# A three-block network on one core: the head steps of the first mixers cut into short pieces, VectorE bound to the planner's order, products placed behind every second dense step, and weights beyond seven fetched later

## The chip, the core and the metric

The kernel runs on one core of a Trainium2 chip, in one launch. What counts is the time of that core on the device, in microseconds (us). Engines: TensorE (PE in the profile; PEld is its weight load), VectorE (DVE), ScalarE (ACT), GpSimd (POOL) and SyncE (SP), which issues the weight transfers.

## What is computed

Three blocks follow each other on a sequence of 512 positions with 1024 channels, all in 32-bit floats: a block with two mixers (a gated delta rule on four heads and a retention on four heads) and a convolutional MLP, then a block of sliding-window attention with pooling, then a gated convolution block. The change touches the first mixers, and a little of the passage into the last block.

```python
proj = rms_norm(h, attn_norm_w) @ w_in            # 36 tiles of 128 columns
q, k, v = split(silu(causal_conv4(...)))          # gated delta rule, 4 heads of 128
q, k = l2norm(q) * d**-0.5, l2norm(k)
m = where(strict, (k*beta) @ k.T * decay, 0)      # per chunk
t_mat = solve_triangular(eye + m, eye)            # unit lower triangle
u_base, w_mat = t_mat @ (v*beta), t_mat @ (k*beta*exp(gcum))
qk = (q @ k.T) * decay
# scan over the chunks:
u = u_base - w_mat @ S;  o = (q*exp(gcum)) @ S + qk @ u;  S = S*cd + k_dec.T @ u
o = rms(o) * norm_w * silu(gate)                  # per head
# retention, 4 heads: rotary q, k; o = rms(retention(q, k, v)) * silu(gate)
h = h + concat(o_gdn, o_ret) @ w_out
```

## The kernel before

**Dense products.** Activations lie channels by positions. Each 32-bit factor is split into a high and a low part, and a dense product is three matmuls of 128x512 (`mm3`, lines 330 to 332). A projection tile is eight dense steps (k = 0 to 7) of three matmuls (`side_steps`). Weights come by SP into three buffers (`raw`); ScalarE makes the high part (`whi`, or `op` where buffers are lent), VectorE or GpSimd the low part (`unpack`, `prefetch`).

**First mixers.** While the 36 projection tiles go through TensorE, the heads' own small products are put between the dense steps. A head of the delta rule is a generator, `gdn_head`: sums of squares (L704) and transposes of k (L686); the norms on VectorE (`rsqrt_small`, some ten tiny operations, each needing the one before); the products k·k (L732) and q·k (L734), which VectorE turns into `Mt` and `At` with four SCALAR_TENSOR_TENSOR each; the triangular inverse by doubling, two batches of 16 tiny products (L759) per level with VectorE between them; then the scan over four chunks (L831, L832, L842, L848, L855), in which VectorE makes `ru` and the state. `finish_head` normalizes a head's result, again with a chain of tiny operations, `ret_head` is a retention head.

**The planner.** A loop written in the kernel sets the order. It keeps a clock of its own: a dense step adds 0.64 to it, a head's step adds the cost that it yields, and the step after it is ready once the clock has passed the latency that it yields (`need(n, lat, cost)`; the constants `L_PRE`, `L_NORM`, `L_M` and so on). A ready step goes ahead of the next dense step. The order so made is binding for PE and SP alone (`manual_schedule`); what stands on VectorE, ScalarE and GpSimd is ordered by the framework's scheduler. A step's instructions on an engine run in the order in which they stand there, whatever is ready.

```python
ready = [e for e in live if e[0] <= clock[0]]
if ready: step(ready[0])
elif main ...: clock[0] += next(main)             # one dense step
else: clock[0] = min(e[0] for e in live)
```

**Passage into the last block.** The output product of the second block runs in two halves of the positions; `p6_norm` is a chain of norms for each half (squares, a row sum on TensorE at L1275, a reciprocal root, then 8 tiles scaled), while the first seven tiles of the last block's weights (`N_FIRST`) are used on the other half. `prefetch` takes further weights as buffers come free.

Of the kernel before, what the change touches and what calls it, by code (L numbers as in the profile page):

```python
# [41 lines left out]
L_NORM = 15  # L42
L_M = 5.8
# [113 lines left out]
def build(tc, xT, par, cst, rope, w_ab, w_in, w_rv, w_out, w_up, w_down, a_w, ab_w, c_w, co_w, post1, poolw, out, dbg=None):  # L157
# [134 lines left out]

    def prefetch(ins=None):
# [46 lines left out]
    credit = [0.0]  # L340
# [15 lines left out]
    def side_steps(ws, X, sl=slice(0, T), ab=None):  # L356
# [6 lines left out]
        for k in range(KD):  # L363
# [57 lines left out]
    def rsqrt_small(y, x, n, tag):  # L421


        h, t = small(n, tag + "l"), small(n, tag + "t")
# [8 lines left out]


# [222 lines left out]
    def finish_head(i, scale, wn):  # L657
# [3 lines left out]
        so, ms, r = small(NCH, "so"), small(NCH, "oms"), small(NCH, "or")  # L661
# [3 lines left out]
        fr(junk)  # L665
        if scale is not None:
# [3 lines left out]
        rsqrt_small(r, ms, NCH, "ors")  # L670
# [3 lines left out]
        yield from need(1, L_FIN)  # L674
# [14 lines left out]
    def gdn_head(h, qT, kT, vT):  # L689
# [16 lines left out]
        sse = sp.tile([128, 2, 4], F32, tag="sse", name="sse")  # L706
        rn = sp.tile([128, 2, 4], F32, tag="rn", name="rn")
# [5 lines left out]
        rsqrt_small(rn.rearrange("p a c -> p (a c)"), sse.rearrange("p a c -> p (a c)"), 8, "rn")  # L713
# [13 lines left out]
        pm.fr(pv)  # L727
        fr(vT)
# [8 lines left out]
        for c in range(NCH):  # L737
            STT(At[:, ch(c)], pkq[:, ch(c)], f[:, c:c + 1], Ec[:, ch(c)], MUL, MUL)
        pm.fr(pk, pkk, pkq)
        fr(Ec, Es)  # L740
# [10 lines left out]
        gps.memset(Tf, 0.0)  # L751
        TT(vc(Tt, c32), vc(Mc, c32), bc4(cc("lev", 0, c32)), MUL)
# [9 lines left out]
        cost = 2.2  # L762
        for n in range(1, 5):
            yield from need(1, L_M if n == 1 else L_T, cost)
# [5 lines left out]
            yield from need(1, L_Z, cost)  # L770
# [160 lines left out]

    def step(e):

        try:
            cost, lat = next(e[1])
            clock[0] += cost
            e[0] = clock[0] + lat
        except StopIteration:
# [820 lines left out]
```

## Time and profile before

| what | value |
|---|---|
| median of 3 runs | 1109.29 us (1107.78 to 1110.65) |
| the profiled execution | 1109.99 us, span 1108.2 us |
| PE busy in the span | 1081.0 us, 98% |
| DVE, ACT, POOL busy | 759.6, 508.5, 200.8 us |
| granted TensorE clock, mean | 0.994 of full speed |
| transfers | 96.04 MB, mean 87 GB/s |

The span runs from the first instruction to the last. A busy PE is not a PE at its peak: matmuls are pipelined, each is shown as 0.39 us long while the next starts 0.23 us later, so waits are read from the starts. In a row of the timeline the first number is the start in us from the span's start, the second the duration, then come engine, line, operation, tiles written and read, the shape, the count, and in brackets the idle time before it with what ended it. Lines are those of the kernel before; in the changed kernel they stand 2 to 20 lines further down (L704 is L714, L686 is L696, L732 is L742, L754 is L762, L759 is L767, L709 is L720).

### The profile page before, as it was taken

Reading aid. Unit: us, or ns where it says so; the run is one execution under the profiler, and the core shown is the slowest. Engines: PE = TensorE matmul, PEld = TensorE weight load, DVE = VectorE, ACT = ScalarE, POOL = GpSimd, SP = SyncE. Lnnn points to the kernel's source line nnn. Section 1 sums busy time; section 2 is a strip of 40 time slices with the busy share of each in tenths; the row PEclk is TensorE's granted clock in tenths of the full one; section 3 lists DMA queues with packets and bytes.
Section 4 is the critical chain, followed back from the end, with each engine's and each line's share of the span. In section 5 each row is a group of like instructions: output and inputs, shape, how many; then the busy total and the mean of one; then the engine's idle time right before and its main releaser. Section 6 shows DMA issues by size and latency. Waiting matters only on the chain.

```text
span 1108.2 us, 17712 instructions
## 1 busy us (share of the span) xinstructions
PE 1081.0 (98%) x6902; PEld 871.6 (79%) x6902; DVE 759.6 (69%) x1522; ACT 508.5 (46%) x1017; POOL 200.8 (18%) x194
## 2 busy tenths in 40 slices
PE   7998989999999999999999999999999999999997
PEld 5876778788888888888888888766789996665886
DVE  7787566577567877676663234668855857989855
ACT  6742444215344544443453245355445546544542
POOL 0931222101030000000000016000000003999100
PEclk9998999999999999999999999999999999999999
DMA  8321112114232333333333333211232403111021
GB/s 287 120 78 55 40 59 77 59 38 134 77 114 76 114 95 96 98 104 103 95 96 93 100 96 106 77 58 39 77 95 76 153 23 113 57 59 60 18 76 76
DMA packets 28947, 96.04 MB, mean 87 GB/s; under 512 B 3552, under 2 KB 3808, under 8 KB 28864
## 3 DMA queue, kind: packets, MB, share of 16 engines
q1 hardware_dynamic: 27936, 91.90, 26.3%
q0 software_dynamic: 928, 3.02, 0.9%
q8 instruction: 54, 0.88, 0.3%
q14 instruction: 29, 0.24, 0.1%
HBM read 92.81 MB, written 2.10 MB: 86 GB/s over the span
## 4 chain that ended last, share of the span: by engine, by line
PE 88%; DVE 8%; ACT 1%; DMA 1%; issue 1%; SPq 0%; DVEq 0%; ACTq 0%
PE bank L330 26%; PE bank L331 25%; PE bank L332 25%; DVE act L175 2%; PE bank L1443 2%; DVE act L178 2%; PE bank L1149 1%; PE bank L759 1%; PE bank L1187 1%; DVE bank L178 1%; DVE wlo L175 1%; PE bank L1176 1%; PE bank L1427 1%; PE bank L438 1%; DMA raw<-in_c_w_dram 1%
## 5 line engine op out<-in xcount | busy, mean ns | idle before, releaser
L330 PE MATMUL bank<-op,whi 128*128 128x512 f32 (+1 forms) x575 | 224.1, 390 | 5.8 <-ACT whi L171 5.8
L332 PE MATMUL bank<-op,wlo 128*128 128x512 f32 (+1 forms) x575 | 217.6, 378 | 0.0
L331 PE MATMUL bank<-op,whi 128*128 128x512 f32 (+1 forms) x575 | 217.5, 378 | 0.0
L330 PE MATMUL bank<-op,op 128*128 128x512 f32 (+1 forms) x538 | 207.2, 385 | 0.4 <-ACT stk L171 0.4
L331 PE MATMUL bank<-op,op 128*128 128x512 f32 (+1 forms) x538 | 202.5, 376 | 0.0
L332 PE MATMUL bank<-op,op 128*128 128x512 f32 (+1 forms) x538 | 202.0, 375 | 0.0
L171 ACT ACTIVATE op<-raw 128x512 fp32r<-128x512 f32 (+1 forms) x168 | 102.3, 625 | 144.1 <-PE bank L331 117.2
L171 ACT ACTIVATE whi<-raw 128x512 fp32r<-128x512 f32 (+1 forms) x158 | 96.2, 622 | 127.0 <-PE bank L331 120.5
L175 DVE TENSOR_TENSOR op<-raw,op 128x512 fp32r<-128x512 f32 (+1 forms) x140 | 97.0, 705 | 68.3 <-ACT op L171 67.9
L330 PEld LDWEIGHTS bank<-op,whi 128*128 128x128 f32 x575 | 109.5, 190 | 29.5 <-ACT whi L171 6.0
L332 PEld LDWEIGHTS bank<-op,wlo 128*128 128x128 f32 x575 | 109.4, 190 | 20.4 <-DVE wlo L175 0.4
L331 PEld LDWEIGHTS bank<-op,whi 128*128 128x128 f32 x575 | 109.7, 191 | 19.6 <-issue 1.9
L175 DVE TENSOR_TENSOR wlo<-raw,whi 128x512 fp32r<-128x512 f32 (+1 forms) x129 | 91.8, 717 | 43.6 <-ACT whi L171 43.2
L330 PEld LDWEIGHTS bank<-op,op 128*128 128x128 f32 x538 | 101.5, 189 | 24.4 <-issue 4.3
L332 PEld LDWEIGHTS bank<-op,op 128*128 128x128 f32 x538 | 101.4, 188 | 18.6 <-issue 0.6
L331 PEld LDWEIGHTS bank<-op,op 128*128 128x128 f32 x538 | 101.5, 189 | 17.4 <-issue 1.3
L171 ACT ACTIVATE act<-act 128x512 f32<-128x512 f32 (+3 forms) x113 | 56.2, 506 | 77.3 <-DVE act L175 23.0
L175 POOL TENSOR_TENSOR act<-act,act 128x512 f32<-128x512 f32 x57 | 78.8, 1390 | 28.1 <-ACT act L171 26.6
L175 DVE TENSOR_TENSOR bank<-bank,act 128x512 f32<-128x512 f32 x56 | 38.6, 695 | 52.3 <-PE bank L332 52.1
L330 PE MATMUL bank<-whi,op 128*128 128x512 f32 (+1 forms) x199 | 73.4, 369 | 0.4 <-DVE act L175 0.4
L332 PE MATMUL bank<-whi,op 128*128 128x512 f32 (+1 forms) x199 | 72.6, 365 | 0.0
L331 PE MATMUL bank<-wlo,op 128*128 128x512 f32 (+1 forms) x199 | 72.3, 363 | 0.0
(362 smaller groups left out, 1650.5 us busy)
## 6 DMA issues: line engine op xcount, KB each, us to landing
raw<-in_w_up_dram SPq DMA_DIRECT2D x44, 512.0 KB, 3.5
raw<-in_w_in_dram SPq DMA_DIRECT2D x25, 512.0 KB, 3.6
raw<-in_c_w_dram SPq DMA_DIRECT2D x24, 512.0 KB, 3.7
raw<-in_a_w_dram SPq DMA_DIRECT2D x18, 512.0 KB, 3.4
raw<-in_w_down_dram SPq DMA_DIRECT2D x16, 448.0 KB, 3.3
raw<-in_w_out_dram SPq DMA_DIRECT2D x8, 512.0 KB, 3.5
raw<-in_w_down_dram SPq DMA_DIRECT2D x8, 512.0 KB, 3.5
raw<-in_ab_w_dram SPq DMA_DIRECT2D x8, 512.0 KB, 3.4
```

Of the source, the lines that this page charges most:

```text
L171: last[0] = act.activation(out=out, in_=in_, func=func, **k)
L175: return (e or dve).tensor_tensor(out=out, in0=in0, in1=in1, op=o)
L178: return (e or dve).scalar_tensor_tensor(out=out, in0=in0, scalar=scalar, in1=in1, op0=o0, op1=o1)
L330: pe.matmul(ps, lhsT=l[0], rhs=r[0], start=first, stop=False)
L331: pe.matmul(ps, lhsT=l[0], rhs=r[1], start=False, stop=False)
L332: pe.matmul(ps, lhsT=l[1], rhs=r[0], start=False, stop=last)
L438: pe.matmul(p, lhsT=ones, rhs=ss, start=True, stop=True)
L759: pe.matmul(p[pt(i), c * c32:(c + 1) * c32], lhsT=l[pt(i), c * c32:(c + 1) * c32], rhs=r[pt(i), c * c32:(c + 1) * c32], start=True, stop=True)
L1149: pe.matmul(v2(psc[e])[:, i, lo:], lhsT=qT[sl, ch(b)], rhs=kT[sl, (b - 1) * C + lo:(b + 1) * C], start=True, stop=True)
L1176: pe.transpose(v2(pt)[:, i, ch(j)], sc[:, i, ch(j)], ident)
L1187: pe.matmul(po[64 * e:64 * e + 64, ch(b)], lhsT=vtok[:, kb * C + 64 * e:kb * C + 64 * e + 64], rhs=v2(pT)[:, i, ch(j)], start=j == 0 or b ...
L1443: pe.matmul(acc[32 * q:32 * q + 32], lhsT=wds[m][i // 4][:, i % 4 * C + 32 * q:i % 4 * C + 32 * q + 32], rhs=st[:, o:o + T], start=i == 0, ...
```

## The change

The latencies of two steps are shortened (15 to 4.0 and 5.8 to 2.0). The chains of tiny operations become steps of their own (`rsqrt_steps`), which yield a third number and so count as steps without products. `step` queues each step's VectorE instructions behind those of the step before, so the planner's order binds VectorE for the heads' steps; the evacuations of the dense tiles and the weights' low parts stay with the scheduler. `grain` is true after every second dense step, and a step with products waits for that. In `gdn_head` the product q·k with its four VectorE operations moves from ahead of the inverse into its first level, and v's scaling moves behind the diagonal's preparation. `cap` stops `prefetch` at seven weights of the last block until the second half begins. No product, transfer or element of work is added or taken away; tiny tiles get four buffers where they had two.

```diff
-L_NORM = 15
-L_M = 5.8
+L_NORM = 4.0
+L_M = 2.0
...
-        while nxt[0] < len(stream) and len(his.free) >= 2 * len(landing) + 2 and raws.free:
+        while nxt[0] < cap[0] and len(his.free) >= 2 * len(landing) + 2 and raws.free:
...
@@ side_steps
+            grain[0] = k % 2 == 1 or len(ws) > 1
             yield 0.64 * len(ws)
...
-    def rsqrt_small(y, x, n, tag):
+    def rsqrt_steps(y, x, n, tag, bufs=2):
...
         TT(h, t, x, MUL)
+        yield
         STT(t, h, -10.0 / 3.0, h, ADD, MUL)
...
@@ finish_head
         fr(junk)
+        yield 0.0, 2.2, 0
...
-        rsqrt_small(r, ms, NCH, "ors")
+        for _ in rsqrt_steps(r, ms, NCH, "ors", 4):
+            yield 0.0, 1.2, 0
+        yield 0.0, 1.0, 0
...
-        yield from need(1, L_FIN)
+        yield from need(1, L_FIN - 6.0)
...
@@ gdn_head
+        yield 1.0, 0.4, 0
...
-        rsqrt_small(rn.rearrange("p a c -> p (a c)"), sse.rearrange("p a c -> p (a c)"), 8, "rn")
+        for _ in rsqrt_steps(rn.rearrange("p a c -> p (a c)"), sse.rearrange("p a c -> p (a c)"), 8, "rn", 4):
+            yield 0.0, 2.0, 0
+        yield 0.0, 1.0, 0
...
-        yield from need(3, L_NORM, 2.2)
+        yield from need(2, L_NORM)
...
-        TT(v4(vr), v4(pv), b3(rki), MUL)
...
-        pkk, pkq = pm(), pm()
+        pkk = pm()
...
-        for c in range(NCH):
-            pe.matmul(pkq[:, ch(c)], lhsT=kT[:, ch(c)], rhs=qT[:, ch(c)], start=True, stop=True)
+        yield 1.3, 0.3, 0
...
+        TT(v4(vr), v4(pv), b3(rki), MUL)
...
+            if n == 1:
+                pkq = pm()
...  (q·k and its four VectorE operations)
+            yield from need(1, L_Z, 1.4 if n == 1 else cost)
...
@@ step
+        n = len(tc.nc.cur_bb.bb.instructions)
+        with contextlib.ExitStack() as behind:
+            if turn[0] is not None:
+                behind.enter_context(tc.issue_after(turn[0]))
...
+        for i in tc.nc.cur_bb.bb.instructions[n:]:
+            if i.engine == mybir.EngineType.DVE:
+                turn[0] = i
...
-        ready = [e for e in live if e[0] <= clock[0]]
+        ready = [e for e in live if e[0] <= clock[0] and (grain[0] or not e[3])]
...
+    cap[0] = len(stream) - co_w.shape[0] - c_w.shape[0] + N_FIRST
     start_chain(0)
```

How the order changes is shown at three places. **First, TensorE where heads 0 and 1 make their products of keys.** `bank` is an accumulator, `stk` and `act` are activations, `ck` the identity. Before:

```order
L686 MATMUL bank_165<-ck,stk_95 128x128 x4
L732 MATMUL bank_163<-stk_96 128x128 x4
L734 MATMUL bank_159<-stk_95,stk_96 128x128 x4
L330 MATMUL bank_160<-op_111,whi_143 128x512
L331 MATMUL bank_160<-op_112,whi_143 128x512
L332 MATMUL bank_160<-op_111,wlo_153 128x512
L704 MATMUL bank_165<-act_70,ck 32x128 x4
```

Now:

```order
L696 MATMUL bank_163<-ck,stk_95 128x128 x4
L742 MATMUL bank_165<-stk_96 128x128 x4
L332 MATMUL bank_160<-op_105,whi_143 128x512
L333 MATMUL bank_160<-op_106,whi_143 128x512
L334 MATMUL bank_160<-op_105,wlo_153 128x512
L332 MATMUL bank_160<-op_107,whi_143 128x512
L333 MATMUL bank_160<-op_108,whi_143 128x512
L334 MATMUL bank_160<-op_107,wlo_153 128x512
L696 MATMUL bank_159<-ck,stk_95 128x128 x4
L742 MATMUL bank_162<-act_86 128x128 x4
```

q·k (L734) is gone from behind k·k, six matmuls (two dense steps) stand between the two heads, and both heads' k·k now stand ahead of the sums of head 2. Head 0's first batch of the inverse (L759, now L767) has 78 dense matmuls ahead of it since the tile of q2 began, before and now; its second batch has 87 before and 90 now; head 0's second level begins after 96 in both.

**Second, VectorE ahead of the first batches of the inverse.** `act_76` is head 0's diagonal and the matrices made of it, `act_82` head 1's; `act_75` and `stk_96` are `Mt` of heads 0 and 1, `act_74` is `At` of head 0, `wlo` a weight's low part. Before, up to head 0's transposition (L754):

```order
L175 TENSOR_TENSOR act_73<-bank_165,rki 128x512
L178 SCALAR_TENSOR_TENSOR act_75<-bank_163,f,act_84 128x128 x4
L178 SCALAR_TENSOR_TENSOR act_74<-bank_159,f,act_78 128x128 x4
L175 TENSOR_TENSOR act_76<-act_76,act_93 128x128
L709 STREAM_TRANSPOSE act_70<-bank_165 128x256
L175 TENSOR_TENSOR act_76<-act_76,ck 128x128
L175 TENSOR_TENSOR wlo_152<-raw_136,whi_142 128x512
L754 STREAM_TRANSPOSE act_76<-act_76 128x128
```

Now, up to the same transposition (L762), and then the end of the list up to head 1's:

```order
L178 SCALAR_TENSOR_TENSOR act_75<-bank_165,f,act_85 128x128 x4
L178 SCALAR_TENSOR_TENSOR stk_96<-bank_162,f,act_89 128x128 x4
L175 TENSOR_TENSOR act_76<-act_76,act_93 128x128
L175 TENSOR_TENSOR act_73<-bank_163,rki 128x512
L175 TENSOR_TENSOR act_76<-act_76,ck 128x128
L175 TENSOR_TENSOR bank_160<-bank_160,act_67 128x512
L762 STREAM_TRANSPOSE act_76<-act_76 128x128
```

```order
L175 TENSOR_TENSOR act_76<-bank_162,act_93 128x128
L178 SCALAR_TENSOR_TENSOR act_74<-bank_163,f,act_78 128x128 x4
L175 TENSOR_TENSOR act_82<-act_82,act_93 128x128
L175 TENSOR_TENSOR stk_96<-bank_159,rki 128x512
L175 TENSOR_TENSOR act_82<-act_82,ck 128x128
L178 SCALAR_TENSOR_TENSOR rnt<-rnl 128x8
L175 TENSOR_TENSOR wlo_154<-raw_137,whi_144 128x512
L762 STREAM_TRANSPOSE act_82<-act_82 128x128
```

`At` of head 0 (made of q·k), the sums of head 2 (L709) and one low part have moved from ahead of head 0's transposition to behind it; `Mt` of head 1 and an evacuation (`bank_160`) have moved ahead of it. Between the two lists stand head 2's sums, that low part, three operations of a convolution and five tiny ones.

**Third, VectorE in the scan, where heads finish.** `or`, `orst`, `orsl` are the tiny tiles of `finish_head`, `rn`, `rnt` those of head 3's norms; the row with `neg` makes `ru`, which TensorE's next product awaits. Before:

```order
L178 SCALAR_TENSOR_TENSOR orst<-orst,oms 128x4
L175 TENSOR_TENSOR orst<-or 128x4
L178 SCALAR_TENSOR_TENSOR rn<-rnt,rn 128x8
L178 SCALAR_TENSOR_TENSOR or<-orst,or 128x4
L178 SCALAR_TENSOR_TENSOR orst<-orst,oms 128x4
L175 TENSOR_TENSOR rnt<-rn 128x8
L175 TENSOR_TENSOR or<-or,cq 128x4
L178 SCALAR_TENSOR_TENSOR or<-orst,or 128x4
L178 SCALAR_TENSOR_TENSOR rnt<-rnt,sse 128x8
L175 TENSOR_TENSOR act_89<-act_89,or 128x512
L178 SCALAR_TENSOR_TENSOR rn<-rnt,rn 128x8
L178 SCALAR_TENSOR_TENSOR stk_95<-bank_165,neg,act_78 128x128
```

Now:

```order
L175 TENSOR_TENSOR stk_95<-stk_95,bank_163 128x128
L175 TENSOR_TENSOR rki<-sse,rn 128x4
L175 TENSOR_TENSOR f<-rn 128x4
L182 TENSOR_SCALAR cq<-rn 128x4
L175 TENSOR_TENSOR f<-f,beta 128x4
L175 TENSOR_TENSOR fl<-f,ge 128x4
L175 TENSOR_TENSOR stk_96<-bank_165,fl 128x512
L175 TENSOR_TENSOR so<-so,cq 128x4 x2
L182 TENSOR_SCALAR oms<-so 128x4
L182 TENSOR_SCALAR orst<-oms 128x4
L182 TENSOR_SCALAR or<-orst 128x4
L175 TENSOR_TENSOR orst<-or 128x4
```

Before, two finishing heads and head 3's norms lie interleaved ahead of one `ru`; now they come one after the other, half a chain at a time, with the scan's operations between the pieces.

## Rows read from the trace of the kernel before

**Rows 1.** The page: busy time by engine, its share of the span, and instructions.

```profile
PE 1081.0 (98%) x6902; PEld 871.6 (79%) x6902; DVE 759.6 (69%) x1522; ACT 508.5 (46%) x1017; POOL 200.8 (18%) x194
```

**Rows 2.** Waits of TensorE over the whole span: line, what ended them, us in total, times, longest.

```profile
PE bank L759 <- DVE act L175: 4.4, 1, 4.4
PE bank L842 <- DVE f L175: 3.6, 1, 3.6
PE bank L1275 <- DVE act L175: 2.0, 1, 2.0
PE bank L704 <- ACT act L171: 1.5, 2, 1.2
PE bank L759 <- DVE act L776: 1.2, 1, 1.2
PE bank L759 <- issue: 0.5, 1, 0.5
```

**Rows 3.** Stretches of the span: from and to, length, busy us (and instructions) of PE, PEld, DVE, ACT and POOL, then the granted clock, the share of the DMA engines and GB/s.

```profile
60.50:81.40 20.90, 19.36 (x136) 16.02 (x135) 18.74 (x56) 8.48 (x16) 5.75 (x6) 1.00 0.23 73
84.40:88.80 4.40, 0.10 (x1) 0.00 (x0) 4.40 (x23) 2.95 (x7) 0.71 (x2) 0.79 0.00 2
88.80:93.80 5.00, 4.95 (x59) 3.56 (x62) 2.51 (x6) 0.03 (x1) 0.93 (x1) 0.50 0.31 108
105.90:120.00 14.10, 12.43 (x401) 9.64 (x387) 10.58 (x28) 4.58 (x10) 4.07 (x10) 1.00 0.27 78
153.90:158.60 4.70, 0.73 (x4) 0.30 (x2) 4.70 (x22) 1.61 (x2) 2.11 (x3) 1.00 0.00 0
158.60:162.10 3.50, 3.44 (x11) 2.86 (x11) 1.93 (x6) 0.80 (x2) 0.00 (x0) 0.51 0.45 145
874.00:890.00 16.00, 13.96 (x112) 13.60 (x111) 12.67 (x33) 5.88 (x15) 0.00 (x0) 1.00 0.54 165
```

**Rows 4.** TensorE's timeline where heads 0 and 1 make their products.

```profile
74.02 1.06 PE L732 MATMUL bank<-stk 128*128 128x128 f32 x8
74.91 1.06 PE L734 MATMUL bank<-stk,stk 128*128 128x128 f32 x8
...
81.78 0.45 PE L759 MATMUL bank<-act 32*32 32x32 f32 x32
...
83.88 0.39 PE L331 MATMUL bank<-op,whi 128*128 128x512 f32 x1
84.11 0.39 PE L332 MATMUL bank<-op,wlo 128*128 128x512 f32 x1
88.85 0.65 PE L759 MATMUL bank<-act 32*32 32x32 f32 x32 [4.36 <-DVE act L175]
...
93.57 0.63 PE L759 MATMUL bank<-act 32*32 32x32 f32 x41
```

**Rows 5.** VectorE's timeline in the same stretch.

```profile
76.07 2.15 DVE L178 SCALAR_TENSOR_TENSOR act<-bank,f,act 128x128 f32<-128x128 f32 x8
...
79.73 1.35 DVE L175 TENSOR_TENSOR wlo<-raw,whi 128x512 fp32r<-128x512 f32 x1 [0.35 <-ACT whi L171]
81.00 0.30 DVE L754 STREAM_TRANSPOSE act<-act 128x128 f32<-128x128 f32 x1
...
83.85 0.74 DVE L178 SCALAR_TENSOR_TENSOR stk<-bank,pr,stk 128x510 f32<-128x510 f32 x1
...
88.32 0.28 DVE L175 TENSOR_TENSOR act<-act,act 128x128 f32<-128x128 f32 x1
88.52 0.28 DVE L175 TENSOR_TENSOR act<-bank,act 128x128 f32<-128x128 f32 x1
88.72 1.16 DVE L175 TENSOR_TENSOR act<-act,ck 128x128 f32<-128x128 f32 x1
```

**Rows 6.** GpSimd's timeline in this stretch.

```profile
88.39 1.34 POOL L175 TENSOR_TENSOR wlo<-raw,whi 128x512 fp32r<-128x512 f32 x1 [3.10 <-ACT whi L171]
```

**Rows 7.** VectorE's timeline in the scan.

```profile
151.96 1.20 DVE L175 TENSOR_TENSOR rnt<-rn 128x8 f32<-128x8 f32 x1
...
157.31 0.33 DVE L178 SCALAR_TENSOR_TENSOR stk<-bank,neg,act 128x128 f32<-128x128 f32 x1
```

**Rows 8.** ScalarE's timeline in the scan.

```profile
149.22 1.28 ACT L171 ACT_TABLE_LOAD   x1
150.52 0.60 ACT L171 ACTIVATE act<-bank 128x512 f32<-128x512 f32 x1
...
151.48 0.31 ACT L171 ACTIVATE act<-stk 128x128 f32<-128x128 f32 x1
151.70 0.19 ACT L171 ACTIVATION_READ_ACCUMULATOR act<-stk 128x1 f32 x1
```

**Rows 9.** VectorE's timeline in the passage into the last block, second half of the positions.

```profile
879.10 0.17 DVE L175 TENSOR_TENSOR qt<-qy 128x8 f32<-128x8 f32 x1
879.30 0.17 DVE L175 TENSOR_TENSOR qt<-qt,qx 128x8 f32<-128x8 f32 x1
...
881.80 1.29 DVE L175 TENSOR_TENSOR op<-raw,op 128x512 fp32r<-128x512 f32 x2 [2.14 <-ACT op L171]
883.02 0.44 DVE L455 STREAM_TRANSPOSE act<-qy 128x256 f32<-128x256 f32 x1
883.49 6.32 DVE L175 TENSOR_TENSOR act<-act,act 128x256 f32<-128x256 f32 x18
```

More of the change, by code (lines that the diff above doesn't have):

```diff
@@ L291, in unpack @@
         made.append(w)
+    cap = [len(stream)]
     def prefetch(ins=None):
@@ L338, in build @@
     pend = collections.deque()
-    credit = [0.0]
+    credit, grain = [0.0], [True]
     def tick(n=RATE):
@@ L419, in rsqrt_guess @@
         TS(y.bitcast(I32), t.bitcast(I32), -1.0, MUL, float(0x5F3759DF), ADD)
-    def rsqrt_small(y, x, n, tag):
-        h, t = small(n, tag + "l"), small(n, tag + "t")
+    def rsqrt_steps(y, x, n, tag, bufs=2):
+        h, t = small(n, tag + "l", bufs), small(n, tag + "t", bufs)
         rsqrt_guess(y, x, t)
@@ L432, in rsqrt_small @@
         STT(y, t, 9.0 / 16.0, y, ADD, MUL)
+    def rsqrt_small(*a):
+        for _ in rsqrt_steps(*a):
+            pass
     def row_sums(ss):
@@ L660, in finish_head @@
         o, scale = O[i], scale and scale()
-        so, ms, r = small(NCH, "so"), small(NCH, "oms"), small(NCH, "or")
+        so, ms, r = (small(NCH, n, 4) for n in ("so", "oms", "or"))
         junk = al()
@@ L705, in gdn_head @@
         pk = transpose4(kT)
-        sse = sp.tile([128, 2, 4], F32, tag="sse", name="sse")
-        rn = sp.tile([128, 2, 4], F32, tag="rn", name="rn")
+        sse = sp.tile([128, 2, 4], F32, tag="sse", name="sse", bufs=4)
+        rn = sp.tile([128, 2, 4], F32, tag="rn", name="rn", bufs=4)
+        yield 1.0, 0.4, 0
         st = sq[0][:, :256]
@@ L722, in gdn_head @@
         TT(v4(kd), v4(pk), b3(fl), MUL)
-        yield from need(3, L_NORM, 2.2)
+        yield from need(2, L_NORM)
         pv = transpose4(vT)
         vr = al()
-        TT(v4(vr), v4(pv), b3(rki), MUL)
-        pm.fr(pv)
-        fr(vT)
         At, Mt = al(), al()
-        pkk, pkq = pm(), pm()
+        pkk = pm()
         for c in range(NCH):
             pe.matmul(pkk[:, ch(c)], lhsT=kT[:, ch(c)], rhs=kT[:, ch(c)], start=True, stop=True)
-        for c in range(NCH):
-            pe.matmul(pkq[:, ch(c)], lhsT=kT[:, ch(c)], rhs=qT[:, ch(c)], start=True, stop=True)
+        yield 1.3, 0.3, 0
         for c in range(NCH):
             STT(Mt[:, ch(c)], pkk[:, ch(c)], f[:, c:c + 1], Es[:, ch(c)], MUL, MUL)
[L737 to L740, printed above, removed]
+        pm.fr(pk, pkk)
+        fr(Es)
         c32, g4 = C // 4, range(4)
@@ L751, in gdn_head @@
         gps.memset(Tf, 0.0)
+        yield 0.0, 2.8, 0
         TT(vc(Tt, c32), vc(Mc, c32), bc4(cc("lev", 0, c32)), MUL)
@@ L760, in tiles @@
                               rhs=r[pt(i), c * c32:(c + 1) * c32], start=True, stop=True)
-        cost = 2.2
+        TT(v4(vr), v4(pv), b3(rki), MUL)
+        pm.fr(pv)
+        fr(vT)
+        cost = 0.0
         for n in range(1, 5):
-            yield from need(1, L_M if n == 1 else L_T, cost)
+            yield from need(2 if n == 1 else 1, L_M if n == 1 else L_T, cost)
             cost = 0.5
@@ L769, in gdn_head @@
             pm.fr(pz)
-            yield from need(1, L_Z, cost)
+            if n == 1:
+                pkq = pm()
+                for c in range(NCH):
+                    pe.matmul(pkq[:, ch(c)], lhsT=kT[:, ch(c)], rhs=qT[:, ch(c)], start=True, stop=True)
+                for c in range(NCH):
+                    STT(At[:, ch(c)], pkq[:, ch(c)], f[:, c:c + 1], Ec[:, ch(c)], MUL, MUL)
+                pm.fr(pkq)
+                fr(Ec)
+            yield from need(1, L_Z, 1.4 if n == 1 else cost)
             pb = pm()
@@ L930, in start @@
         wait.append((g, key, after))
+    turn = [None]
     def step(e):
[L934 to L938, printed above, removed]
-            live.remove(e)
-            if e[2] is not None:
-                done.add(e[2])
+        n = len(tc.nc.cur_bb.bb.instructions)
+        with contextlib.ExitStack() as behind:
+            if turn[0] is not None:
+                behind.enter_context(tc.issue_after(turn[0]))
+            try:
+                cost, lat, *vec = next(e[1])
+                clock[0] += cost
+                e[3] = not vec
+                e[0] = clock[0] + lat
+            except StopIteration:
+                live.remove(e)
+                if e[2] is not None:
+                    done.add(e[2])
+        for i in tc.nc.cur_bb.bb.instructions[n:]:
+            if i.engine == mybir.EngineType.DVE:
+                turn[0] = i
     def admit():
@@ L948, in admit @@
                 wait.remove(x)
-                live.append([0.0, x[0], x[1]])
+                live.append([0.0, x[0], x[1], False])
                 step(live[-1])
@@ L1033, in build @@
                 main = None
+                grain[0] = True
         else:
             clock[0] = min(e[0] for e in live)
+            grain[0] = True
     order.close()
@@ L1370, in p7_units @@
                 lazy[0] = False
+                cap[0] = len(stream)
                 order.close()
```

1 line of the change is left out of this document (added).

## Prediction

> **What bounds the kernel now.** I read the page first: TensorE is busy 98% of the span [rows 1], so only its waits, its clock and the room between its matmuls can give time. The list of its waits comes next [rows 2]. The change reaches six of them: 4.4 and 1.2 us at the batches of the inverse (L759) and 0.5 more there, 3.6 at the scan (L842), 1.5 in two waits at the sums (L704), and 2.0 at the row sum of the passage into the last block (L1275). Third, the stretches [rows 3]: the 4.4 us wait is followed by 5.0 us at a granted clock of 0.50, the wait at L842 by 3.5 us at 0.51, which is the lower of the two levels. All other rows of the stretches, with waits of 1.2, 0.5 and 2.0 us in them, have 1.00. So a long wait is paid twice: about 5.0 x 0.5 = 2.5 us behind the first, 3.5 x 0.49 = 1.7 behind the second. Fourth, who makes TensorE wait: in both long waits VectorE is busy for the whole stretch (4.40 of 4.40 and 4.70 of 4.70), and from 60.5 to 81.4 it is busy 18.74 of 20.90 [rows 3]. VectorE, not TensorE, sets the pace between about 60 and 91 us. That is what the reader should take along: an order on TensorE helps there only as far as VectorE's list up to the awaited result gets shorter.
>
> **The change part by part.** No work is added, so each term is a wait that goes or comes. I follow VectorE's list to the next result that TensorE awaits.
>
> *Head 0's first batch.* Before, VectorE ends the transposition at 81.30 [rows 5] and TensorE starts the batch at 81.78 without a wait [rows 4]. Now the list up to it lacks four of eight SCALAR_TENSOR_TENSOR (2.15 / 8 = 0.27 each, 1.07), a low part (1.27, from 79.73 to 81.00 [rows 5]) and a transposition of 256 columns (0.44 shown [rows 9], 0.36 with the overlap below). It has four more of head 1's `Mt` (1.07) and an evacuation of 512 columns, like a low part that nothing hinders (0.6). Net: 1.0 shorter. A part of VectorE's own idle time is filled too; I take 0.4. So the result is ready near 79.9. TensorE comes earlier by more: two q·k (0.89 each by k·k's starts, 74.02 to 74.91 [rows 4]) stand behind this point now, and the 1.5 us at L704 [rows 2] belong to a silu that VectorE finishes sooner against TensorE's order. It would be there at 81.8 - 1.8 - 1.5 = 78.5. New wait: 1.4, in one piece or split with the sums of head 2.
>
> *Head 1's first batch.* Behind it VectorE has, in order: a transposition 0.44, a low part 0.68, three conv operations of 0.74 [rows 5], five tiny ones of which two hide (3 x 0.20, by the starts 879.10 and 879.30 [rows 9]), the level's mask 0.28, `At` 1.07, three of 0.28, 0.68 and 0.28 for head 1, a tiny one, a low part 0.68 and the transposition 0.30. That is 7.7 as shown; operations start about 0.08 before the one ahead is shown to end (88.32 + 0.28 against 88.52 [rows 5]), 14 times, so 6.6. GpSimd makes two low parts meanwhile. Its operation at 88.39 took 1.34 [rows 6], and a VectorE operation that began at 88.72 then took 1.16 where two like it took 0.28 [rows 5]: 0.9 lost. Two such make 1.8 at most, none at least. I take 1.1, so 7.7: ready at 87.6 (86.5 to 88.3). TensorE has a batch 0.45, q·k 0.89, twelve dense matmuls at 0.23 (83.88 to 84.11 [rows 4]) and a batch, 4.6 in all, and is there at 84.5. New wait: 3.1 (2.0 to 3.8). After it a batch, q·k and six dense matmuls, 2.7, bring head 0's second level to 90.3. Before, that level began at 93.57 [rows 4] with the same 96 dense matmuls and both q·k behind it, and head 1's batch (0.45) still to come. Gain 3.7, if the clock stays up. A wait of 3.1 lies between the 2.0 that left the clock at 1.00 and the 4.4 and 3.6 that did not, nearer to 3.6. So in the forecast it falls, and I charge 2.1, the middle of 2.5 and 1.7. **Gain here 1.6** (1.0 to 4.5).
>
> The Trainium skill (SBUF — State Buffer, section "Who interferes with whom") says that VectorE's second read interface is shared with GpSimd and locked for a whole instruction: a VectorE operation with two inputs in SBUF waits until a GpSimd operation that reads SBUF has ended, or the other way round. The 1.16 us beside the 1.34 us agree. By the page alone each GpSimd operation can cost up to its full 1.34 us; for the five of the two stretches that is up to 6.7 in place of the some 2 us in my terms, and the sum would come out at a gain near 2.
>
> *Later levels.* Between 93.8 and 120 the two waits of 1.2 and 0.5 [rows 2] stood behind VectorE's convolution and norm operations. Now every result there has two or four dense steps (1.4 or 2.7 us) of TensorE's time to be made in, against one to three operations of 0.2 to 0.74. **Gain 1.7** (0.5 to 1.7).
>
> *The scan.* Before, `ru` at 157.31 [rows 7] had some thirty tiny operations of three chains ahead of it, one of them 1.20 long under a GpSimd operation [rows 7]. Its wait, 3.6 at L842 and 0.4 before the next dense matmul, 4.70 - 0.73 = 4.0 by the stretch, and the clock's 1.7 go [rows 3]: 5.7. What comes: ScalarE's list holds two Squares (0.31 and 0.19 each), a silu like the 0.60 of a 512-column row, the table load 1.28, an exponential 0.60 and a copy 0.3 [rows 8], 3.8, against 3.8 of TensorE's (decays, sums, transposes, a piece of the scan, two dense steps): 0 to 0.7 wait; three more Squares then 0.3; VectorE's piece of head 3's norms and of a finish ahead of `ru`, twelve tiny ones at 0.20 and one of 0.68, 3.1, against 1.7 of TensorE's and a head start of some 0.5: 0.9, and up to 2 with a GpSimd operation in it; an accumulator that comes free late, 0.4. With the clock kept, since dense steps lie between them, 2.5 (1.5 to 4.5). **Gain 3.2** (1.2 to 4.2).
>
> *The passage.* Before, two low parts wait 2.14 for a transfer, and the transposition at 883.02, ready since about 879.7, stands behind both; then 18 operations lead to the awaited row sum [rows 9]. Now one low part stands behind the transposition and one among the 18. The chain starts 0.6 (one low part) plus 0.5 (the transposition no longer in it) sooner and carries one low part more: 0.5 off the 2.0 wait of L1275. SP's order of transfers is the same, so `cap` moves nothing else. **Gain 0.5** (0 to 1.1).
>
> *New small waits.* The chains in pieces run one after another (0.20 per operation where interleaved ones overlapped), so later batches of head 3 can come late: ten tiny ones and two of 0.68, some 3.4 to 4, against 3.2 of TensorE's. **Loss 0.5** (0 to 1.5).
>
> **Sum:** 1.6 + 1.7 + 3.2 + 0.5 - 0.5 = 6.5. The profiled execution took 1109.99, 0.7 above the median of 1109.29; 1109.99 - 6.5 gives **1103.5 us**. By the bounds alone: 1109.99 - 11.5 = 1098.5, and 1109.99 - 1.2 = 1108.8.
>
> **The rivals.**
> 1. *The clock stays up at the inverse.* The 2.1 are not paid: 1101.4. For it: the wait is shorter than both that cost the clock, and VectorE's time may be at its lower bound. Against: between 83.9 and 89 TensorE has one small batch and no dense matmul, much as before.
> 2. *VectorE's backlog only moves.* GpSimd's operations cost as much as they can, or the waits go from two places to five: gain some 2.5, 1107.5. For it: VectorE is full from 60 to 91 and keeps the same work.
> 3. *Nothing awaited is late any more.* All of 4.4, 3.6, 0.4, 1.5, 1.2, 0.5 and the clock's 4.2 gone, and the passage's 0.5: 16.3, so 1093.7. Against it stand the two lists above, both longer than TensorE's time.
> 4. *Slower: the clock falls through both stretches of short waits.* Before, two solid waits; now some eight of 0.3 to 3 us, with two dense steps between. If they keep TensorE at the lower level from the first wait near 78 to 96, and again over some 20 us of the scan, dense matmuls there go at half speed and take some 0.2 more each: 24 and 36 of them, 12 us on top of rival 1's 1101.4, so 1113.4. It decides if short waits between dense steps cost the clock as the long ones did. Against it: 14.1 us with waits of 1.2 and 0.5 kept 1.00 [rows 3].
>
> The Trainium skill (TensorE: Matmul & The Clock Gate, section "A second HAM failure mode: psum-queue depth-cycling") tells of a kernel whose many short idle times between groups of matmuls let the clock swing between its two levels; that rule is rival 4. The stretch of 105.9 to 120 does not bear it out.
>
> **How the numbers follow.** The forecast has 0.42, rival 1 0.26, rival 2 0.15, rival 3 0.08, rival 4 0.09. A measurement of this kernel can tell about 0.3%, 3.3 us, from no change, so faster means below 1106.0. Forecast, rivals 1 and 3 make 0.76, less 0.03 for the upper end of the forecast's own spread (1101 to 1106.5): 0.73 faster; rival 2 with that rest 0.18 the same; 0.09 slower. The range goes from 1097.5, below rival 1's best bound, to 1108.5, above rival 2; it leaves out rivals 3 and 4 and little else.
>
> **What would show it.** Right: no wait over 3.5 us in the first mixers; the longest at head 1's first batch of the inverse (L767), 2 to 4 us, still put down to VectorE; at the scan several waits under 1.5 us and a granted clock of 1.00 there; the wait at the passage 1.4 to 1.6. Head 0's second level starts near 90 after the same 96 dense matmuls. Wrong: VectorE idle over 3 us between 60 and 88 (then its order itself holds it up); a clock of 0.50 in the scan; or a new wait outside these two stretches.

## The result and the profile after

The changed kernel takes 1102.3 us (median of 4 runs, 1101.44 to 1103.67) against 1109.82 for the one before: a ratio of 0.994, interval 0.9927 to 0.9952. Five further runs gave 1102.21, ratio 0.9942 (0.9929 to 0.9954). By these medians the gain is 7.5 us here and 6.3 in the further runs (1108.46 before). Of the run `clumped` below, one execution of four took 4050.61 us, and its median is that of the other three. The profiled execution took 1101.57 in a span of 1099.8. Its busy time answers to [rows 1]:

```profile
PE 1078.9 (98%) x6902; PEld 868.9 (79%) x6902; DVE 760.8 (69%) x1522; ACT 507.4 (46%) x1017; POOL 199.9 (18%) x194
```

The work is the same on every engine. The waits of TensorE, against [rows 2]:

```profile
PE bank L767 <- DVE rn L178: 3.4, 1, 3.4
PE bank L742 <- DVE stk L178: 1.0, 1, 1.0
PE bank L767 <- DVE act L795: 0.7, 1, 0.7
PE bank L874 <- ACT act L171: 0.6, 1, 0.6
...
PE bank L767 <- DVE act L175: 0.5, 1, 0.5
...
PE bank L861 <- DVE stk L178: 0.5, 1, 0.5
PE bank L1307 <- DVE act L175: 0.4, 1, 0.4
```

One long wait is left, at head 1's first batch of the inverse (L767). The 3.6 at the scan has become three of 0.5 to 1.0 (L874, L861, and L742 in the middle of it), the 2.0 of the passage is 0.4 (L1307), the 1.5 at the sums is gone. The stretches, columns as in [rows 3]:

```profile
60.50:78.40 17.90, 17.90 (x121) 14.20 (x119) 17.02 (x56) 9.18 (x20) 5.24 (x5) 1.00 0.29 89
83.70:87.10 3.40, 0.01 (x2) 0.03 (x2) 3.37 (x11) 0.58 (x2) 1.27 (x1) 1.00 0.01 2
87.80:91.20 3.40, 3.40 (x13) 2.96 (x12) 2.84 (x12) 0.00 (x0) 0.30 (x1) 0.50 0.50 154
92.00:106.00 14.00, 13.26 (x342) 10.62 (x346) 12.25 (x34) 4.29 (x9) 1.60 (x2) 1.00 0.14 41
148.00:162.00 14.00, 11.97 (x80) 9.56 (x73) 11.31 (x42) 7.51 (x27) 4.80 (x5) 1.00 0.13 39
```

VectorE is busy for the whole of the long wait (3.37 of 3.40), 3.4 us at 0.50 follow it, and the scan now has 1.00. TensorE's timeline shows the batches of [rows 4]:

```profile
78.49 0.45 PE L767 MATMUL bank<-act 32*32 32x32 f32 x32
...
83.25 0.45 PE L767 MATMUL bank<-act 32*32 32x32 f32 x32 [0.49 <-DVE act L175]
87.10 0.45 PE L767 MATMUL bank<-act 32*32 32x32 f32 x32 [3.39 <-DVE rn L178]
...
91.55 0.45 PE L767 MATMUL bank<-act 32*32 32x32 f32 x32
```

Head 0's first batch starts without a wait, head 1's waits 3.39, head 0's second level starts at 91.55 where it was 93.57. The long waits before and now are not those of one batch: the 4.36 of [rows 4] stood at head 0's second batch (88.85), which now waits 0.49 (83.25), and head 1's first batch, which before came together with head 0's second level (93.57), now comes ahead of it and waits. VectorE's timeline up to these two results, and GpSimd's beside the second:

```profile
68.50 0.57 DVE L178 SCALAR_TENSOR_TENSOR rnt<-rnl 128x8 f32<-128x8 f32 x1
...
69.59 0.72 DVE L178 SCALAR_TENSOR_TENSOR rn<-rnt,rn 128x8 f32<-128x8 f32 x1
...
78.04 0.30 DVE L762 STREAM_TRANSPOSE act<-act 128x128 f32<-128x128 f32 x1
...
84.15 1.10 DVE L175 TENSOR_TENSOR act<-act,act 128x128 f32<-128x128 f32 x1
...
86.65 0.30 DVE L762 STREAM_TRANSPOSE act<-act 128x128 f32<-128x128 f32 x1
```

```profile
83.83 1.27 POOL L175 TENSOR_TENSOR wlo<-raw,whi 128x512 fp32r<-128x512 f32 x1 [4.09 <-ACT whi L171]
```

The wait's label names `rn`, the row that starts as the transposition of 86.65 ends. The operation at 84.15 takes 1.10 where the same one in [rows 5] takes 0.28. Last, VectorE in the passage, against [rows 9]: the transposition now stands right behind `qy`, and one low part waits 0.30 where two waited 2.14.

```profile
873.11 0.17 DVE L178 SCALAR_TENSOR_TENSOR qy<-qt,qy 128x8 f32<-128x8 f32 x1
873.31 0.45 DVE L462 STREAM_TRANSPOSE act<-qy 128x256 f32<-128x256 f32 x1
874.06 0.69 DVE L175 TENSOR_TENSOR op<-raw,op 128x512 fp32r<-128x512 f32 x1 [0.30 <-ACT op L171]
```

**A ledger.** Every trace holds all 6902 matmuls, 4320 of them dense, so the start of the same dense matmul can be compared between kernels. The 840th (counted from 0) lies behind all of the first mixers: 298.08 before, 291.71 now, 6.37 sooner. The 2940th, ahead of the passage, is 6.77 sooner, the 3540th, behind it, 8.41. So in this pair of traces the first mixers gave 6.4, the passage 1.6, and 0.4 came between. One trace is one execution: the second trace of the changed kernel gives 5.3, 2.1 and 0.4, and `cap_alone`, which changes nothing in the first mixers, differs by 0.5 there. The table gives this for all runs ("840th": against before; waits and time at the lower clock: between the 120th and the 840th).

| run | median us | ratio to before (95%) | 840th | waits | low clock |
|---|---|---|---|---|---|
| before | | | 0 | 11.6 | 10.2 |
| changed | 1102.30 | 0.994 (0.9927-0.9952) | -6.4 | 7.1 | 3.4 |
| changed_again | 1102.21 | 0.9942 (0.9929-0.9954) | -5.3 | 7.1 | 6.8 |
| cap_alone | 1108.38 | 0.999 (0.9981-0.9999) | -0.5 | 11.2 | 10.2 |
| vector_free | 1100.02 | 0.9916 (0.9903-0.993) | -6.6 | 7.6 | 0 |
| every_step | 1109.79 | 1.0005 (0.9996-1.0013) | +0.1 | 11.2 | 0 |
| head1_later | 1104.69 | 0.9958 (0.9946-0.9971) | -3.9 | 8.7 | 6.8 |
| gps_memset | 1097.31 | 0.9894 (0.988-0.9907) | -12.5 | 3.5 | 0 |
| lat_alone | 1113.13 | 1.0036 (1.0023-1.0048) | +4.3 | 14.9 | 10.2 |
| whole_chains | 1105.50 | 0.9973 (0.9963-0.9982) | -1.5 | 8.8 | 6.8 |
| lob_dve | 1098.35 | 0.9905 (0.9891-0.992) | -10.2 | 5.0 | 0 |
| lob_dve_free | 1100.24 | 0.992 (0.9906-0.9934) | -10.7 | 4.9 | 0 |

The changed kernel's two traces have the same waits, but 3.4 and 6.8 us at the lower clock, and their 840ths lie 1.04 apart. Of the 6.8 us, 1.4 lie inside the long wait (it begins at 85.70, the wait ends at 87.13), where TensorE has nothing to lose.

### The profile page after: what moved, and what is told of

Same layout as the page of the kernel before. It is cut to its first block, busy times and chain, and to the rows that moved or that the text cites. A ratio compares the mean times of both kernels' runs of the same rounds, so it can differ in the third digit from the quotient of the medians.

```text
span 1099.8 us, 17697 instructions
## 1 busy us (share of the span) xinstructions
PE 1078.9 (98%) x6902; PEld 868.9 (79%) x6902; DVE 760.8 (69%) x1522; ACT 507.4 (46%) x1017; POOL 199.9 (18%) x194
## 4 chain that ended last, share of the span: by engine, by line
PE 83%; DVE 10%; ACT 4%; issue 1%; DMA 1%; POOL 1%; SPq 0%; DVEq 0%; POOLq 0%; ACTq 0%
PE bank L332 24%; PE bank L333 23%; PE bank L334 23%; DVE act L175 2%; PE bank L1477 2%; DVE act L178 2%; ACT act L171 1%; DVE wlo L175 1%; PE bank L1181 1%; PE bank L1219 1%; DVE bank L178 1%; ACT whi L171 1%; PE bank L767 1%; DVE op L175 1%; ACT op L171 1%
## 5 line engine op out<-in xcount | busy, mean ns | idle before, releaser
L171 ACT ACTIVATE act<-act 128x512 f32<-128x512 f32 (+3 forms) x108 | 53.8, 507 | 53.5 <-POOL act L175 20.1
```

The source lines that it names most:

```text
L171: last[0] = act.activation(out=out, in_=in_, func=func, **k)
```

## The experiments

The letters A to K are the theories and rivals that the expectations name.

**cap_alone**: the limit on fetched weights put into the kernel before.

```diff
-        while nxt[0] < len(stream) and len(his.free) >= 2 * len(landing) + 2 and raws.free:
+        while nxt[0] < cap[0] and len(his.free) >= 2 * len(landing) + 2 and raws.free:
...
+    cap[0] = len(stream) - co_w.shape[0] - c_w.shape[0] + N_FIRST
     start_chain(0)
...
```

> The kernel before with one edit: no more than seven weights of the last block are fetched until the second half begins. TensorE's and SP's orders stay; on VectorE only the passage changes (the transposition of the norm comes ahead of the two low parts). Theory A (lists: a wait of TensorE lasts until the list of the engine that makes the awaited result has reached it, so each part of the change pays where it shortens such a list, and the parts add up): the wait of 2.0 us at the row sum L1275 falls to about 0.4, the first mixers keep their waits of 4.4 and 3.6, the time falls by 1.6 to 1108.2. Theory C (the transfer that the low part waited 2.14 us for ends that wait whatever the order is): wait 1.5 to 2.0, time 1109.3 or more. The recorded term of 0.5 lies between.

Measured: 1108.38, 1.1 less than before (by the interval 0.1 to 2.1). The wait at the row sum has left the list; the first mixers keep theirs:

```profile
PE bank L761 <- DVE act L175: 4.4, 1, 4.4
PE bank L844 <- DVE f L175: 3.5, 1, 3.5
```

A holds, C falls: SP's order of transfers is the same, and the wait is gone once the transposition no longer stands behind the two low parts. The edit also moves the times of the transfers: ScalarE starts the high part that the low part behind `qy` needs 1.5 us after `qy` ends before (881.14 against 879.67), and as `qy` ends here (878.76). So it is not shown that VectorE's order would have been enough by itself.

**vector_free**: VectorE left to the scheduler.

```diff
-            if i.engine == mybir.EngineType.DVE:
+            if False:
                 turn[0] = i
```

> The changed kernel without the binding of VectorE: the planner sets TensorE's order as in the changed kernel (one place late in the first mixers differs), the framework's scheduler sets VectorE's. Theory A (lists): the chains of tiny operations lie interleaved again ahead of what the scan awaits; a wait of 2 to 4 us comes back in the scan and perhaps the lower clock behind it, so 2 to 5 us slower than the changed kernel, 1104 to 1107. Theory B (switches: the first mixers gain because TensorE changes between dense and small products less often, 64 groups of small products in place of 71): the grouping is the same, so the time is within 1 us of the changed kernel, 1101.5 to 1103.5.

Measured: 1100.02, 2.3 below the changed kernel (2.2 below its further runs). A fails here: no wait comes back in the scan, and the longest are these.

```profile
PE bank L767 <- DVE stk L795: 1.3, 1, 1.3
PE bank L767 <- DVE rnt L178: 1.3, 1, 1.3
PE bank L714 <- ACT act L171: 0.9, 1, 0.9
```

At head 1's first batch the wait is 1.3, not 3.4, and the granted clock's mean was 0.999 in each of five runs (0.995 to 0.998 in four of the changed kernel). Waits in sum are alike (7.6 and 7.1), so the binding does not pay by itself; what it costs is the one long wait, with the clock behind it. The medians show this and the traces hardly do (840th: -6.6 and -6.4), because the profiled execution was the slowest of the five here (1101.67) and one of the faster ones of the changed kernel.

**every_step**: products allowed behind every dense step.

```diff
-            grain[0] = k % 2 == 1 or len(ws) > 1
+            grain[0] = True
...
-                grain[0] = c % 2 == 1
+                grain[0] = True
```

> The changed kernel with steps that hold products allowed behind every dense step, not every second one. Up to the end of the first mixers there are 85 groups of small products between dense matmuls in place of 75 (83 in the kernel before). Theory A (lists): what counts is VectorE's list ahead of each awaited result; head 0's first batch of the inverse now stands three dense steps later, and results have one dense step (0.7 us) less to be made in at each of the later levels and in the scan, so waits of 0.3 to 1 us at many of them: 1 to 4 us slower, 1103.5 to 1106.5, with the loss in the list of waits. Theory B (switches): ten groups more give back all of what the first mixers gained, about 6 us: 1108, with the loss between the matmuls and not in the list of waits.

Measured: 1109.79; the whole gain is gone, by both theories' shares: waits are 4.1 longer, many and most of them short (below), and the 840th is 2.4 later beyond that, though the clock does not fall in the first mixers.

```profile
PE bank L861 <- DVE stk L178: 2.1, 1, 2.1
PE bank L767 <- DVE stk L175: 1.9, 1, 1.9
PE bank L696 <- DVE act L178: 1.6, 1, 1.6
```

**clumped and spread**: is it the changes between dense and small products? Each of 20 tiles of the second block gets 16 products more, in one group or in four; TensorE's order is bound there in both.

```diff
...
+            if extra and k == 7:            # spread: k % 2 == 1, range(4)
+                for i in range(16):
+                    pe.matmul(extra[0][:, ch(i % 4)], lhsT=ident, rhs=ident, start=True, stop=True)
...
```

> The changed kernel with 16 small products more (128x128, the unit matrix with itself, not used by anything) in each of 20 projection tiles of the second block, in one group behind the tile's last dense step: 20 groups, 320 products. At about 0.11 us each (eight k.k products took 0.89) they cost about 35 us, for every theory. It is the base of the next run.

> The same 320 products, four behind every second dense step: 80 groups in place of 20, with no result that anyone waits for. Theory B (each change from dense to small products and back costs TensorE about 0.25 us by itself, the price by which the run with 85 groups lost 3 of its 7 us against the one with 73): 60 x 0.25 = 15 us above the run with one group per tile. Theory A (only waits for results count): the same time within 2 us.

Measured: 1173.78 (ratio 1.0589, 1.0573 to 1.0605) and 1176.73 (1.0614, 1.0598 to 1.063). A product cost 0.224, not 0.11: the trace counts two matmuls for each, which I had overlooked. 60 groups more cost 3.0 by the medians and 2.0 by the dense matmuls ahead and behind (840th to 2940th) of the two traces, 0.03 to 0.05 each. That is at or above the 2 us of theory A and far from the 15 of theory B, which falls: a change costs little when the operands are there. What the 2.4 of every_step beyond its waits are stays open.

**head1_later**: two dense steps moved ahead of head 1's first batch.

```diff
-            yield from need(2 if n == 1 else 1, L_M if n == 1 else L_T, cost)
+            yield from need(2 if n == 1 else 1, (3.3 if h == 1 else L_M) if n == 1 else L_T, cost)
```

> The changed kernel with the latency ahead of head 1's first batch of the inverse at 3.3 instead of 2.0: on TensorE two dense steps (six matmuls, 1.4 us) move from behind that batch to ahead of it, and nothing else moves there. Theory A (lists): VectorE reaches the awaited transposition at 86.9 as before, TensorE is there 1.4 later, so the wait falls from 3.4 to 2.0; the granted clock behind it stays at 1.00, because 2.0 lies among the waits that did not lower it; head 0's second level starts up to 2 us earlier: 1 to 2.5 us faster than the changed kernel, 1099.8 to 1101.3. Rival D (the clock falls by what TensorE does around the wait and not by the wait's length): wait 2.0, clock still 0.5 to 0.6 for some 3 us, gain under 1 us. Rival E (head 0's second level is VectorE's next result and is not ready earlier): the wait only moves to it, time within 0.5 us of the changed kernel.

Measured: 1104.69, slower by 2.4. TensorE's timeline, VectorE's, and the stretch of lower clock:

```profile
87.33 0.45 PE L767 MATMUL bank<-act 32*32 32x32 f32 x32 [1.83 <-DVE rn L178]
91.95 0.27 PE L767 MATMUL bank<-act 32*32 32x32 f32 x4 [2.67 <-DVE act L795]
```

```profile
87.16 0.69 DVE L175 TENSOR_TENSOR bank<-bank,act 128x512 f32<-128x512 f32 x1
...
88.70 0.74 DVE L178 SCALAR_TENSOR_TENSOR act<-bank,pr,act 128x511 f32<-128x511 f32 x1
...
91.59 0.30 DVE L795 STREAM_TRANSPOSE act<-act 128x128 f32<-128x128 f32 x1
```

```profile
88.30:95.10 6.80, 4.13 (x50) 3.72 (x48) 4.96 (x18) 1.48 (x3) 1.58 (x2) 0.50 0.20 76
```

The wait fell as A said (3.39 to 1.83), but rival E came true in its mechanism, though not in its time (within 0.5 said): a wait of 2.67 moved to head 0's second level. The two dense steps end a projection tile ahead of this place and no longer behind it, and the scheduler put its evacuation (87.16) and three convolution operations (from 88.70) ahead of the transposition that this level awaits (91.59, where it was 89.22). The clock fell after the wait of 1.83, as D said and A did not; it stayed low for 6.8 us where D said some 3.

**changed_again**: the same kernel, as a base.

> The changed kernel once more, with more runs, as the base for small differences and to settle whether the kernel without the binding of VectorE (1100.02) is really faster. Two readings of its first result: its profiled execution agreed with that of the changed kernel within 0.1 us of span, so either the binding makes no difference and this run gives 1099.5 to 1101, or the binding costs about 2 us through the lower clock behind the 3.4 us wait, which comes in every execution, and this run gives 1101.5 to 1103.

Measured: 1102.21, and the granted clock's mean is 0.995 to 0.997 in all five runs, so the second reading holds. Its profile has the lower clock for longer:

```profile
85.70:92.50 6.80, 5.37 (x62) 4.30 (x66) 4.94 (x22) 0.00 (x0) 0.30 (x1) 0.50 0.27 81
```

**gps_memset**: GpSimd writes zeros in place of its share of the low parts, so this kernel leaves out that part of the computation and GpSimd reads nothing there.

```diff
+            if lo_e[o // 512] is gps and nxt[0] < 80:
+                gps.memset(lo.bitcast(F32)[:, :m], 0.0)
...
```

> The changed kernel, in which GpSimd's share of the low parts of the first weights is replaced by writing zeros (that part of the computation is left out), so GpSimd reads nothing from SBUF there; the orders of VectorE and TensorE are the same. Theory F (VectorE's operations that take 1.1 to 1.35 us in place of 0.3 or 0.7 stand still because GpSimd reads SBUF at that time): the product with the unit matrix at 84.15 falls from 1.10 to 0.28, the low part at 78.94 from 1.35 to 0.68, the tiny ones at 59 to 70 to 0.17; VectorE reaches the transposition of head 1 1.5 to 2.4 us sooner, the wait of 3.4 falls to 1.0 to 1.9, the clock stays at 1.00, and the time is 2 to 4 us below the changed kernel. Rival G (those operations are long for a reason of their own, a semaphore or a transfer): they stay at 1.1 or more, and so do the wait and the time, within 1 us of the changed kernel.

Measured: 1097.31, 4.9 below the changed kernel, beyond F's range. VectorE's rows (the operation of 84.15, and head 1's transposition), then the waits:

```profile
82.47 0.28 DVE L175 TENSOR_TENSOR act<-act,act 128x128 f32<-128x128 f32 x1
...
84.15 0.30 DVE L765 STREAM_TRANSPOSE act<-act 128x128 f32<-128x128 f32 x1
```

```profile
PE bank L770 <- DVE rn L178: 1.9, 1, 1.9
PE bank L864 <- DVE stk L178: 1.1, 1, 1.1
```

1.10 is now 0.28, the transposition comes 2.50 sooner, the wait is 1.9, the clock stays at 1.00. The orders of VectorE and TensorE are those of the changed kernel, so this is shown: GpSimd's low parts make VectorE stand still. At 82.47 GpSimd is idle in this run; what a write does shows where a low part of VectorE's and a write of GpSimd's start together, VectorE's row first:

```profile
131.70 0.69 DVE L175 TENSOR_TENSOR op<-raw,op 128x512 fp32r<-128x512 f32 x1 [1.50 <-ACT op L171]
```

```profile
131.70 0.53 POOL L289 MEMSET op<- 128x512 f32 x1 [0.38 <-PE bank L337]
```

VectorE's low part takes its 0.69 there; beside a low part of GpSimd's (1.27, from 79.26) it took 1.35 (79.73 in [rows 5]). So it is the reads that count. The Trainium skill (SBUF — State Buffer, section "Who interferes with whom") says that a VectorE operation with two inputs in SBUF contends with a GpSimd one that reads SBUF and not with one that only writes it; the 0.69 beside a write and the 1.35 beside a read agree.

**lob_dve and lob_dve_free**: VectorE makes GpSimd's share itself from the tenth tile on; in the second run without the binding.

```diff
-LO_B = (1, 0)
+LO_B = 0, 0
```

> The changed kernel with GpSimd's share of the low parts given to VectorE from the tenth projection tile on (15 operations of 0.68; nothing is left out, TensorE's order is the same). Theory F (a GpSimd operation that reads SBUF stops VectorE for up to its 1.3 us): VectorE takes each low part for 0.60 and gets back 0.4 to 0.8 that it stood still, so its list ahead of head 1's first batch changes by less than 0.5 and the time by less than 1 us: 1101.2 to 1103.2. Rival K (GpSimd's help was worth its full time to VectorE): two low parts more ahead of that batch, 1.2 to 1.4 us, waits of 4.6 there and more at the later levels, 2 to 4 us slower than the changed kernel: 1104 to 1106.

> The same without the binding of VectorE, as in the run of 1100.02. If theory F and the cost of the binding add up: 1099 to 1101, within 1 us of that run; if VectorE's spare time there was used up already (rival K): 1102 to 1104.

Measured: 1098.35 and 1100.24. The first is 3.9 below the changed kernel, more than F said (less than 1); K falls. Waits of lob_dve:

```profile
PE bank L767 <- DVE act L762: 1.7, 1, 1.7
PE bank L767 <- DVE rn L178: 1.6, 1, 1.6
```

The 3.4 has become two, at head 0's and head 1's first batches, and the clock stays up. The two effects do not add: without the binding nothing more is gained. The second run's 1100.24 lies in the range of the first reading (1099 to 1101), but that reading took the low parts alone to gain next to nothing.

**lat_alone**: the two latencies in the kernel before.

```diff
-L_NORM = 15
-L_M = 5.8
+L_NORM = 4.0
+L_M = 2.0
```

> The kernel before with the two shorter latencies alone (15 to 4.0 and 5.8 to 2.0): the heads' steps come sooner on TensorE, but products stand behind every dense step, the chains are whole, VectorE is left to the scheduler. Theory A (lists and reserve: a wait is what VectorE's list up to a result exceeds TensorE's work up to its use): TensorE now has both heads' products and head 0's first batch of the inverse without a dense matmul between them, while VectorE has 16 operations of 0.27 us for Mt and At (4.3 us) to make; the 4.4 us wait moves to this batch and the scan keeps a wait of 3 us or more: 1108 to 1112, no gain. Rival H (the latencies are the part of the change that pays, because the inverse starts sooner): 3 us or more of the gain: 1106.5 or less.

Measured: 1113.13, slower than before by more than A's range, and H falls. In place of the 4.4 stand 1.7 (q·k, L734) and 2.3 (L759), and the scan keeps a long wait:

```profile
PE bank L759 <- DVE act L754: 3.0, 2, 2.3
PE bank L842 <- DVE act L178: 2.6, 1, 2.6
```

**whole_chains**: each chain of tiny operations in one step.

```diff
-            yield 0.0, 1.2, 0
-        yield 0.0, 1.0, 0
+            pass
+        yield 0.0, 2.2, 0
...
```

> The changed kernel with each chain of tiny operations in one piece again (the latencies of its pieces are summed into one behind it; on TensorE some groups move by one or two dense steps). Theory A (lists): up to ten more tiny operations of 0.20 us stand ahead of an awaited result, above all ahead of ru in the scan, whose waits were 0.60, 0.47 and 0.97: 0.5 to 2.5 us slower than the changed kernel, 1102.7 to 1104.7. Rival J (the pieces pay nothing, since the run without the binding, where the scheduler mixed the chains as it liked, had no long wait in the scan): within 0.7 of the changed kernel, 1101.5 to 1102.9.

Measured: 1105.5, 3.3 slower than the changed kernel, beyond A's range; J falls. The wait for `ru` (L861) is 2.1 where it was 0.5, and another of 2.3 stands at a batch behind the scan; the clock falls once behind that and once near 80, after waits of 0.54 and 1.37.

```profile
PE bank L767 <- DVE or L175: 2.3, 1, 2.3
PE bank L861 <- DVE stk L178: 2.1, 1, 2.1
```

## Why the prediction was nearly right

The forecast of 1103.5 and the measured 1102.3 differ by 1.2. The sum was to be 6.5 and is 8.4 between the profiled executions (a slower one of the kernel before and a faster one of the changed); by the medians it is 7.5 and 6.3. By its own steps:

- **Head 0's first batch.** TensorE was there at 78.49 (78.5 said), but no wait of 1.4 came: VectorE's transposition starts at 78.04 and not near 79.6. The step that failed is the list's size: 1.4 shorter said, 2.96 measured (81.00 to 78.04). I followed the operations that moved and took what stands ahead of 73 us as unchanged. There two tiny operations had taken 1.15 and 1.27 beside GpSimd before (the rows below, of the kernel before); now two others take 0.57 and 0.72, 1.1 less in sum. The other 0.5 of the miss is open.

```profile
68.40 1.15 DVE L175 TENSOR_TENSOR rki<-sse,rn 128x4 f32<-128x4 f32 x1
...
69.55 1.27 DVE L182 TENSOR_SCALAR cq<-rn 128x4 f32<-128x4 f32 x1
```

- **Head 1's first batch.** Right, and for the reason given: ready at 87.6 said, 86.95 measured; a wait of 3.1 said, 3.39 measured (and 0.49 ahead of it), put down to VectorE. That both numbers are so near is in part luck. The list from head 0's transposition to head 1's took 8.6 (78.34 to 86.95) where 7.7 was said, 1.5 of it beside GpSimd (0.67 at the low part of 78.94, 0.82 at 84.15) where I took 1.1, and it began 1.6 sooner. The clock fell as said, and the 2.1 that I charged was about right: the batch, q·k and six dense matmuls behind the wait were to take 2.7 and took 4.45 (87.10 to 91.55), so 1.75, and 2.45 in the second trace:

```profile
87.13 0.65 PE L767 MATMUL bank<-act 32*32 32x32 f32 x32 [3.39 <-DVE rn L178]
...
92.28 0.54 PE L767 MATMUL bank<-act 32*32 32x32 f32 x32
```

  Gain at head 0's second level: 1.6 said; 93.57 - 91.55 = 2.0 measured, and with head 1's batch (0.45), which the prediction counts in, 2.5. That the length of the wait tells whether the clock falls was a reading from two waits only: over all runs a wait of 1.83, or 0.54 and 1.37, was followed by the lower clock, and 1.94 or 2.1 was not. Its length alone does not decide, and what does is open. Nor did the clock fall only behind the wait: the row of the 4.4 us wait itself has 0.79 [rows 3].
- **Later levels.** 1.7 said; one wait of 0.74 is left of 1.7, so 1.0.
- **The scan.** Waits of 2.5 said, 0.60 + 0.47 + 0.97 = 2.04 measured, the clock at 1.00: 5.7 - 2.0 = 3.7 against 3.2. The size is right, the reason only in part. I had the binding keep the chains apart; without it the scan is as good, while whole chains under the binding bring the wait for `ru` back. So it is the pieces that pay there and not the binding.
- **The passage.** 0.5 said, 1.6 measured, beyond the bound of 1.1. The failed step: I let the chain start 1.1 sooner (0.6 for a low part, 0.5 for the transposition) and carry one low part more, and left the 2.14 that the low parts wait for a transfer in it. With the transposition first, this wait lies beside the chain: 0.20 from `qy` (873.11) to the transposition, where it was 3.52 (to 883.02 from the row below, of the kernel before). That `cap` moves nothing else did not hold either: the transfers come at other times.

```profile
879.50 0.17 DVE L178 SCALAR_TENSOR_TENSOR qy<-qt,qy 128x8 f32<-128x8 f32 x1
```

- **New small waits.** 0.5 said; outside those counted above there is one of 0.16 (L687, at 278.46). But 2.5 + 1.0 + 3.7 + 1.6 is 8.8, and 8.4 was measured, so about as much as the term was lost where the list of waits shows next to nothing. What took it is open.

**Rivals:** 1 (the clock stays up) is the run without the binding and lob_dve, not this kernel. 2 fell, since VectorE's list up to head 0's first batch got 2.96 shorter; but at the inverse a long wait did move, from head 0 to head 1, and is 1.0 shorter. 3 fell: 7.1 us of waits are left. 4 fell in this kernel: the clock was low for 3.4 and 6.8 us where it had been 10.2. What I did not see at all is the weight of the spacing of two dense steps: without it, at these latencies, the rest gains nothing in sum. No run has the spacing alone in the kernel before, or the move of q·k alone, so what each is worth by itself is not shown.

## What to carry to other kernels

Where TensorE waits for a busy engine, count that engine's list up to the awaited result, operation by operation, and count in it the time that it stands still beside another engine; work given to a helper can cost the helped engine more than doing it itself, as it did here (0.82 lost against 0.69). A result needs a reserve of TensorE's work between its making and its use: two dense steps paid here, and one gave all of it back. Before a step is moved to fill a wait, look at what the scheduler will put into the place that it leaves.

## What the runs showed of the hardware

A GpSimd low part of 128x512 took 1.27 and held VectorE's 128x128 product up by 0.82 (1.10 against 0.28), while VectorE makes the same low part in 0.69; giving 15 of them back to VectorE gained 3.9 us. A tiny TENSOR_SCALAR with one input was held up too: 1.27 at 69.55 above, until a GpSimd low part (69.49 to 70.79) had ended, where the same one at 63.49, alone, took 0.16. A low part of VectorE's beside a GpSimd operation that only writes took its usual 0.69. Four groups of four small products between dense ones cost 0.03 to 0.05 us per added group more than one group of sixteen. And the same kernel, with the same waits, had the lower clock for 3.4 us in one execution and 6.8 in another.
